# A ring of its own for the modulation weights, and squares on ScalarE, in a two-layer RWKV / band-attention trunk

## The chip, the cores and the metric

The kernel runs on one core of a Trainium2 chip. That core has a matrix engine (TensorE, "PE" in the profile, with "PEld" for its weight loads), three engines for everything else (VectorE "DVE", ScalarE "ACT", GpSimd "POOL") and a queue engine (SyncE, "SP") that issues nearly all transfers from the chip's memory. Each engine works through its own instructions in a fixed order and waits on semaphores. The metric is the device time of one execution in microseconds (us), less is better.

## The reference, cut to what matters

All arithmetic is in float32 on 256 tokens (T) with 2048 features (D). Layer 0 is an RWKV-7 time mix and an MLP, layer 1 a banded attention and an MLP. Every sub-layer is normed and modulated by vectors that come from `c`:

```python
for layer in range(DEPTH):
    mod = c @ w_ada[layer] + b_ada[layer]                     # 2048 x 12288 weights for six vectors
    sh1, sc1, gt1, sh2, sc2, gt2 = jnp.split(mod, 6, axis=-1)
    if layer == N_A_LAYERS:
        sh_kv, sc_kv = jnp.split(c @ w_ada_kv + b_ada_kv, 2, axis=-1)
        h_kv = modulate(rms_norm(x, g_kv), sh_kv, sc_kv)
        ...                                                   # shared keys and values
    h = modulate(rms_norm(x, g_mix[layer]), sh1, sc1)
    y = rwkv7_time_mix(...) if layer < N_A_LAYERS else chunk_band_attention(...)
    x = x + gt1[:, None, :] * y
    h = modulate(rms_norm(x, g_mlp[layer]), sh2, sc2)
    x = x + gt2[:, None, :] * sq_relu_mlp(h, w_up[layer], w_down[layer])
return rms_norm(x, g_final)

def sq_relu_mlp(h, w_up, w_down):
    return jnp.square(jax.nn.relu(h @ w_up)) @ w_down         # 2048 -> 8192 -> 2048
```

The modulation vectors are products of one row with large matrices: 14 vectors of 2048, each from 16 MB of weights that are used once.

## The kernel before, in words

**Layout and precision.** Activations stand with features on the 128 partitions and tokens along the free dimension, in 16 tiles of 128 x 256. A float32 product is made of reduced-precision (fp32r) parts: weights and activations are each split into a high half H and a low half L, and a product is H·H + H·L + L·H. A projection (128 output features) takes 16 contraction steps. `proj2` (L390 to L398) does a step in two matmuls: H of the weight against both halves of the activation at once (512 columns, L396), L of the weight against the high half (256 columns, L397). `proj` (L379 to L388) does it in three.

**Weights.** `weight` (L376) loads a projection's weights as two raw tiles of 128 x 1024 (512 KB). `raw` (L348) takes the tile from the ring `raw` and issues the load on SP (L352). `halves` (L355) makes H with a ScalarE cast (L362, tile `wH`) and L with a VectorE subtraction (L365, tile `wL`); both rings have `W_BUFS` = 3 tiles. The ring `raw` has `RAW_BUFS` = 6 tiles. A raw tile is free again when its subtraction is done.

**Modulation.** `ada_work` (L411) is a generator. For each half of a vector it takes 16 steps; a step loads a raw tile of 128 x 1024 modulation weights from the same ring `raw`, and VectorE adds it, scaled by one entry of `c`, to the accumulator `acc` (L423 for the first, L425 for the others). There is one `acc`. After 16 steps `ada_sum` (L432) sums it over the partitions with 32 small matmuls (L437), and VectorE adds the bias (L441). `ada` takes a step, `ada_tick` (L944) one or two per projection, and `ada_need` all that are left for the vectors named. So the steps are strewn between the projections.

**Stages** in the order of time of the profiled execution: layer A with its modulation, to about 760 us; the drain of its last head pairs, in which the output projection `w_o` is begun, and the rest of `out_proj` (L845), to about 840; MLP 0 to about 1586; `attention` (L948) with the shared keys, values and queries to about 1930; its output projection, to about 2040; MLP 1 to the end. The last modulation vector is done at about 2120.

**The MLP** (L883) has four rounds of 16 up and 16 down projections. For an up projection `sum2` (L878) adds the two halves of the PSUM result (a ScalarE copy L880 and a VectorE add L881); then VectorE makes the square of the positive part in one instruction (L904), ScalarE casts it to the high half of the hidden tile `hHL` (L905), and VectorE subtracts for the low half (L906). The first `RAW` = 4 ups of a layer work on activations that are not normed yet; `late_norm` (L527) corrects them, with the maximum in it, and L899 squares. A down projection ends in two VectorE updates of the residual `x` (L931). In the last round `scaled` (L511: L515 on ScalarE, L516 on VectorE) and `ss_add` (L477) prepare the next norm, and `rstd` (L486 to L499) and `normed_tile` (L502: L506 to L508) follow at the next stage's start.

**Attention.** `scores` (L994) loads a head's bias tile, blanks two blocks of it on GpSimd (L1000, L1001), makes the scores in PSUM, and VectorE writes scaled scores plus bias to `s` (L1006), on which the softmax works (L1010 to L1015); `weighted` transposes and multiplies with the values. A pair of heads is worked on between the quarters of a later query projection.

**What sets the order.** The program text names the work; a scheduler (the Tile framework) then sets the order of each engine's instructions before the kernel runs, from the text's order and its own estimate of when operands and buffers come free. SP's loads are in that order too. With one ring, loads stand in the order of the text, since they take its tiles in turn.

Of the kernel before, what the change touches and what calls it, by code (L numbers as in the profile page):

```python
# [2 lines left out]

# [1 line left out]

# [19 lines left out]
C = 64  # L25
# [4 lines left out]
HK = 8  # L30
# [295 lines left out]
class Body:  # L326
# [18 lines left out]
        return self.vecs[:, i, :] if kt is None else self.vecs[:, i, kt:kt + 1]  # L345


    def raw(self, src, shape=None):  # L348
        t = self.wp.tile([P, HK * P], F32, tag="raw", bufs=self.RAW_BUFS, name="raw")
        if shape is not None:  # L350
            t = t.rearrange("p (a b) -> p a b", a=shape)
        self.nc.sync.dma_start(out=t, in_=src)  # L352
        return t
# [57 lines left out]
    def ada_work(self, layer, part):  # L411
        nc = self.nc
        w, bias = self.ada_src(layer, part)
        dst = self.mods[(layer, part)]
        n_ = HK * P
        for half in range(KT // HK):
            self.fin(HK)
            acc = self.wp.tile([P, n_], F32, tag="acc", bufs=1, name="acc")
            for kt in range(KT):
                raw = self.raw(w[kt * P:(kt + 1) * P, half * n_:(half + 1) * n_])  # L420
                ck = self.ct[:, kt:kt + 1]
                if kt == 0:
                    nc.vector.tensor_scalar(out=acc, in0=raw, scalar1=ck, scalar2=0.0, op0=ALU.mult, op1=ALU.add)  # L423
                else:
                    nc.vector.scalar_tensor_tensor(out=acc, in0=raw, scalar=ck, in1=acc, op0=ALU.mult, op1=ALU.add)  # L425
# [113 lines left out]
    def run(self):  # L539
        nc, tc, d = self.nc, self.tc, self.d  # L540
        ctx = self.ctx
        gp = self.gp = ctx.enter_context(tc.tile_pool(name="gp", bufs=1))
        self.wp = ctx.enter_context(tc.tile_pool(name="wp", bufs=2))
        nc.scalar.preload_act_table_set("natural_log_exp_and_others")
        self.hp = ctx.enter_context(tc.tile_pool(name="hp", bufs=2))
        self.csts = gp.tile([P, CST.shape[1]], F32, name="csts")
        self.vecs = gp.tile([P, len(VECS), KT], F32, name="vecs")
        self.bada = gp.tile([P, 2 * 96 + 32], F32, name="bada")
        self.ct = gp.tile([P, KT], F32, name="ct")
        nc.scalar.dma_start(out=self.ct, in_=d["c"])  # L550
# [5 lines left out]
        self.lazy, self.fins = False, iter(())  # L556
        self.ada_done = set()
        self.adas = self.ada_all()

        sv, sp = ExitStack(), ExitStack()  # L560
        v = self.layer_a(sv, sp)
        with ExitStack() as st:
            self.np = st.enter_context(tc.tile_pool(name="npl", bufs=1, side="right", reuse_waits="tile"))
            xp = st.enter_context(tc.tile_pool(name="xp", bufs=1, side="right", reuse_waits="tile"))
            self.x = xp.tile([P, KT, T], F32, name="x")
            for j in range(KT - 2, KT):
                self.split(self.y_hl, j, v[:, j, :])
            sv.close()
            self.ada_need((0, 2), (0, 4), (0, 3))
            nxt = self.out_proj(self.pp, "w_o", self.y_hl, (0, 2), "g_mlp0", (0, 4), (0, 3), self.o_ps)  # L570
            sp.close()
            with ExitStack() as s2:
                pp = s2.enter_context(tc.tile_pool(name="ps_m0", bufs=2, space=bass.MemoryType.PSUM, reuse_waits="tile"))
                self.psm = lambda: pp.tile([P, 512], F32, tag="m", bufs=2, name="m")
                nxt = self.mlp(s2, pp, 0, *nxt, "g_kv", ("kv", 1), ("kv", 0))
            with ExitStack() as s2:
                pp = s2.enter_context(tc.tile_pool(name="ps_at", bufs=2, space=bass.MemoryType.PSUM, reuse_waits="tile"))
                self.psm = lambda: pp.tile([P, 512], F32, tag="m", bufs=1, name="m")
                o_hl = self.attention(s2, pp, *nxt)
                self.ada_need((1, 2), (1, 4), (1, 3))  # L580
                nxt = self.out_proj(pp, "attn_w_o", o_hl, (1, 2), "g_mlp1", (1, 4), (1, 3))
            with ExitStack() as s2:
                pp = s2.enter_context(tc.tile_pool(name="ps_m1", bufs=2, space=bass.MemoryType.PSUM, reuse_waits="tile"))
                self.psm = lambda: pp.tile([P, 512], F32, tag="m", bufs=2, name="m")
                self.mlp(s2, pp, 1, *nxt)
                r = self.rstd()
                for lo, hi, eng in ((0, 4, nc.vector), (11, 14, nc.gpsimd), (4, 8, nc.vector), (8, 11, nc.vector),
                                    (14, KT, nc.gpsimd)):
                    x = self.x[:, lo:hi, :]
                    eng.tensor_tensor(out=x, in0=x, in1=r.unsqueeze(1).to_broadcast([P, hi - lo, T]), op=ALU.mult)  # L590
                    (nc.sync if eng is nc.vector else nc.scalar).dma_start(out=d["out"][:, lo:hi, :], in_=x)
# [291 lines left out]
    def mlp(self, st, pp, layer, scaled, gain, shift, g=None, sc=None, sh=None):  # L883


        nc, tc, d = self.nc, self.tc, self.d
        hp = st.enter_context(tc.tile_pool(name=f"hid{layer}", bufs=1, reuse_waits="tile"))

        rstd, hl, nxt = self.rstd(), self.new_hl(), None

        def up(q, f):
            w = self.weight(d["w_up"][layer, q * KT + f])
            ps = pp.tile([P, 512], F32, tag="pj", bufs=3, name="pj")
            t = hp.tile([P, T], F32, tag="t", bufs=2, name="t")
            h = hp.tile([P, 2, T], F32R, tag="hHL", bufs=18, name="hHL")
            if q == 0 and f < RAW:
                self.proj(ps[:, :TE], w, lambda kt: scaled[:, kt])
                self.late_norm(t, ps, rstd, ALU.max, 0.0)
                nc.vector.tensor_tensor(out=t, in0=t, in1=t, op=ALU.mult)  # L899
            else:  # L900
                ps = ps.rearrange("p (i t) -> p i t", i=2)
                self.proj2(ps, w, lambda kt: hl[:, kt, :, 0:T])
                self.sum2(t, ps)
                nc.vector.scalar_tensor_tensor(out=t, in0=t, scalar=0.0, in1=t, op0=ALU.max, op1=ALU.mult)  # L904
            nc.scalar.copy(h[:, 0, :], t)  # L905
            nc.vector.tensor_tensor(out=h[:, 1, :], in0=t, in1=h[:, 0, :], op=ALU.subtract)  # L906
            hid.append(h)
            if q or f >= RAW:
                self.ada_tick(layer)

        for q in range(NQ):
# [13 lines left out]
            for n in range(KT):  # L925
                w = self.weight(d["w_down"][layer, q * KT + n])
# [3 lines left out]
                for i in range(2):  # L930
                    nc.vector.scalar_tensor_tensor(out=x, in0=ps[:, i, :], scalar=self.mods[(layer, 5)][:, n:n + 1],  # L931
                                                   in1=x, op0=ALU.mult, op1=ALU.add)
# [15 lines left out]
    def attention(self, st, pp, scaled, kv_gain, kv_shift):  # L948
        nc, tc, d = self.nc, self.tc, self.d
        pk = st.enter_context(tc.tile_pool(name="pat", bufs=1, reuse_waits="tile"))  # L950
# [35 lines left out]
        none = lambda: None  # L986
        turn = none
        for j in range(KT):
            t = pk.tile([P, T], F32, tag="vf", bufs=2, name="vf")
            projected(d["w_v_shared"][j], hkv, t, 1, (none, none, turn))  # L990
            turn = lambda j=j, t=t: token_major(j, t)
        o_hl = self.new_hl()
        rb = d["rb"]
        def scores(j, q):  # L994
            out = []
            for hd in range(2):
                K = slice(C * hd, C * hd + C)
                bias = pk.tile([P, 384], F32, tag="bias", bufs=4, name="bias")
                nc.sync.dma_start(out=bias, in_=rb[2 * j + hd])
                nc.gpsimd.memset(bias[0:C, C:P], -1e30)  # L1000
                nc.gpsimd.memset(bias[0:C, 320:384], -1e30)  # L1001
                S = pp.tile([P, 512], F32, tag="S", bufs=2, name="S")
                nc.tensor.matmul(S[:, 0:P], q[K, 0:P], ks[K, j, 0:P], start=True, stop=True)
                nc.tensor.matmul(S[:, P:384], q[K, P:T], ks[K, j, :], start=True, stop=True)
                s = pk.tile([P, 384], F32, tag="s", bufs=4, name="s")
                nc.vector.scalar_tensor_tensor(out=s, in0=S[:, 0:384], scalar=C ** -0.5, in1=bias,  # L1006
                                               op0=ALU.mult, op1=ALU.add)
                m = pk.tile([P, 4], F32, tag="mx", bufs=4, name="mx")
                for i, (lo, hi) in enumerate(((0, P), (P, 384))):
# [121 lines left out]
```

## Time and profile before

| | us |
|---|---|
| median of three runs | 2769.86 |
| lowest, highest | 2765.64, 2773.61 |
| the profiled execution's own time | 2776.48 |
| its span (first to last instruction) | 2774.7 |
| PE busy | 2666.3 |
| DVE busy | 2120.3 |
| ACT busy | 1277.1 |
| POOL busy | 286.7 |

The mean granted clock of TensorE in that execution is 0.986. Busy time counts instructions that work; waiting and issuing does not count. A row of a view of waits reads "who waited <- for what: us in total, times, longest". A row of the groups of lines reads "line, engine, operation, out<-in, shape, count | busy us, mean ns of one | idle us before it <- what ended that". A row of the timeline begins with its start and its length in us; what stands in brackets is the idle time before it and what ended it. Lines are those of the kernel before.

### The profile page before, as it was taken

The numbers are of one execution on the slowest core, as the hardware profiler recorded it, in microseconds if no ns is written. First come the engines' busy times: TensorE is split into PE (matmuls) and PEld (weight loads), VectorE is DVE, ScalarE is ACT, GpSimd is POOL, SyncE is SP. The second block draws the span as 40 slices with busy tenths as digits, with TensorE's granted clock in tenths as the row PEclk, the third lists the DMA queues.
The fourth block names the chain that finished last, engine by engine and source line by source line (L and its number), as shares of the span: only waits on it lengthen the run. The fifth ranks groups of instructions, "written<-read, shape, count | busy, mean of one in ns | idle before, by whom it ended". The sixth has DMA issues, their size and how long they took to land.

```text
span 2774.7 us, 58075 instructions
## 1 busy us (share of the span) xinstructions
PE 2666.3 (96%) x23594; PEld 2236.9 (81%) x23594; DVE 2120.3 (76%) x3161; ACT 1277.1 (46%) x2253; POOL 286.7 (10%) x416
## 2 busy tenths in 40 slices
PE   6999999999999999999999999998999999999997
PEld 3677777777888888888888888776888888888886
DVE  4568678788899888788888997799997566565665
ACT  2345455555445434344344454465454344443454
POOL 0003343353210000000000100000100000000002
PEclk9999999999999999999999999999999999999999
DMA  9876456554686889898898878888867555555553
GB/s 300 279 268 193 153 184 190 169 182 150 211 303 226 304 304 304 292 308 306 299 313 288 294 245 278 277 264 271 282 229 269 184 189 188 185 189 185 187 188 123
DMA packets 217389, 662.62 MB, mean 239 GB/s; under 512 B 21409, under 2 KB 68897, under 8 KB 217121
## 3 DMA queue, kind: packets, MB, share of 16 engines
q1 hardware_dynamic: 215056, 656.36, 71.3%
q8 instruction: 185, 3.03, 0.4%
q10 hardware_dynamic: 2064, 2.54, 0.3%
q14 instruction: 84, 0.68, 0.1%
HBM read 656.72 MB, written 2.10 MB: 237 GB/s over the span
## 4 chain that ended last, share of the span: by engine, by line
PE 79%; DVE 7%; DMA 6%; issue 4%; ACT 2%; POOL 1%; DVEq 0%; ACTq 0%; POOLq 0%
PE pj L396 41%; PE pj L397 21%; DMA raw<-w_ada 3%; DVE wL L365 3%; DMA raw<-w_ada_kv 2%; PE iv L105 2%; PE gr L99 1%; DVE acc L425 1%; PE m L639 1%; PE o L385 1%; PE ms L99 1%; ACT wH L362 1%; POOL sL L117 1%; PE o L387 1%; PE py L320 1%
## 5 line engine op out<-in xcount | busy, mean ns | idle before, releaser
L396 PE MATMUL pj<-aHL,wH 128*128 128x512 f32 x3520 | 1282.1, 404 | 8.7 <-ACT wH L362 6.5
L362 ACT CAST wH<-raw 128x1024 fp32r<-128x1024 f32 x772 | 807.2, 1046 | 973.2 <-PE pj L396 611.2
L365 DVE TENSOR_TENSOR wL<-raw,wH 128x1024 fp32r<-128x1024 f32 x772 | 943.6, 1225 | 270.7 <-ACT wH L362 267.8
L397 PE MATMUL pj<-aHL,wL 128*128 128x256 f32 x3520 | 993.2, 282 | 2.4 <-DVE wL L365 2.3
L396 PEld LDWEIGHTS pj<-aHL,wH 128*128 128x128 f32 x3520 | 666.5, 189 | 170.3 <-issue 10.1
L396 PE MATMUL pj<-hHL,wH 128*128 128x512 f32 x2048 | 725.4, 399 | 4.3 <-DVE hHL L906 4.3
L397 PEld LDWEIGHTS pj<-aHL,wL 128*128 128x128 f32 x3520 | 666.7, 189 | 5.6 <-DVE wL L365 4.0
L397 PE MATMUL pj<-hHL,wL 128*128 128x256 f32 x2048 | 574.6, 281 | 4.8 <-DVE wL L365 4.7
L425 DVE SCALAR_TENSOR_TENSOR acc<-raw,ct,acc 128x1024 f32<-128x1024 f32 x360 | 467.0, 1297 | 123.5 <-DMA raw<-w_ada 83.3
L396 PEld LDWEIGHTS pj<-hHL,wH 128*128 128x128 f32 x2048 | 385.3, 188 | 100.4 <-DVE hHL L906 6.7
L397 PEld LDWEIGHTS pj<-hHL,wL 128*128 128x128 f32 x2048 | 387.4, 189 | 7.1 <-DVE wL L365 6.7
L484 POOL TENSOR_TENSOR ss<-ss,sq 128x256 f32<-128x256 f32 x56 | 52.0, 929 | 1615.5 <-ACT sq L483 1615.2
L931 DVE SCALAR_TENSOR_TENSOR x<-pj,mod,x 128x256 f32<-128x256 f32 x256 | 123.2, 481 | 51.6 <-PE pj L397 48.6
L905 ACT CAST hHL<-t 128x256 fp32r<-128x256 f32 x128 | 51.6, 403 | 61.2 <-DVE t L904 60.2
L639 PE MATMUL m<-rawa,crep 128*32 128x256 f32 x512 | 47.2, 448 | 16.8 <-DMA rawa<-w_ada 16.3
L387 PE MATMUL pj<-aHL,wL 128*128 128x258 f32 x192 | 55.9, 293 | 6.9 <-DVE wL L365 6.9
L385 PE MATMUL pj<-aHL,wH 128*128 128x258 f32 x192 | 56.2, 293 | 2.2 <-ACT wH L362 1.6
L386 PE MATMUL pj<-aHL,wH 128*128 128x258 f32 x192 | 56.3, 293 | 0.0
L906 DVE TENSOR_TENSOR hHL<-t,hHL 128x256 fp32r<-128x256 f32 x128 | 53.4, 417 | 1.4 <-ACT hHL L905 1.4
L904 DVE SCALAR_TENSOR_TENSOR t<-t 128x256 f32<-128x256 f32 x120 | 50.7, 422 | 2.7
L881 DVE TENSOR_TENSOR t<-pj,t 128x256 f32<-128x256 f32 x120 | 50.0, 417 | 0.5 <-ACT t L880 0.5
L241 POOL TENSOR_TENSOR al<-da,csts 128x128 f32<-128x128 f32 x64 | 41.1, 652 | 68.8 <-PE iv L105 64.1
(246 smaller groups left out, 2792.6 us busy)
## 6 DMA issues: line engine op xcount, KB each, us to landing
raw<-w_ada SPq DMA_DIRECT2D x320, 512.0 KB, 4.9
raw<-w_up SPq DMA_DIRECT2D x256, 512.0 KB, 4.8
raw<-w_down SPq DMA_DIRECT2D x256, 512.0 KB, 4.3
rawa<-w_ada SPq DMA_DIRECT2D x64, 512.0 KB, 6.6
raw<-w_ada_kv SPq DMA_DIRECT2D x64, 512.0 KB, 5.6
raw<-w_k SPq DMA_DIRECT2D x32, 512.0 KB, 4.4
raw<-w_r SPq DMA_DIRECT2D x32, 512.0 KB, 4.6
raw<-w_o SPq DMA_DIRECT2D x32, 512.0 KB, 5.0
```

The source lines that it names most:

```text
L99: self.b.nc.tensor.matmul(o(c)[K], lhsT(c)[K], rhs(c)[K], start=True, stop=True)
L105: self.b.nc.tensor.matmul(o[QS[K], c, :], lhsT[QS[R], c, :], rhs[QS[R], c, :], start=True, stop=True, tile_position=(H * R, H * K))
L362: nc.scalar.copy(Hf, raw)
L365: eng.tensor_tensor(out=Lf, in0=raw, in1=Hf, op=ALU.subtract)
L385: nc.tensor.matmul(ps, H[:, i, :], a(kt)[:, 0, :], start=(first and kt == 0), stop=False)
L386: nc.tensor.matmul(ps, H[:, i, :], a(kt)[:, 1, :], start=False, stop=False)
L387: ins = nc.tensor.matmul(ps, L[:, i, :], a(kt)[:, 0, :], start=False, stop=(last and kt == KT - 1))
L396: nc.tensor.matmul(ps, H[:, i, :], a(kt), start=(kt == 0), stop=False)
L397: ins = nc.tensor.matmul(ps[:, 0, :], L[:, i, :], a(kt)[:, 0, :], start=False, stop=(kt == KT - 1))
L425: nc.vector.scalar_tensor_tensor(out=acc, in0=raw, scalar=ck, in1=acc, op0=ALU.mult, op1=ALU.add)
L639: nc.tensor.matmul(ps[g:g + 32, part, :W], crep[:, kt, :], raw[:, i, :], start=(part == 1 and kt < 4), stop=(part == 0 and kt >= KT - 4), ...
L931: nc.vector.scalar_tensor_tensor(out=x, in0=ps[:, i, :], scalar=self.mods[(layer, 5)][:, n:n + 1], in1=x, op0=ALU.mult, op1=ALU.add)
```

## The change

- Modulation steps can take their raw tile from a ring of their own, `rada`. The context `ada_room(n)` opens a pool with `n` such tiles; inside it `raw(..., ada=True)` uses that pool. It is open around the first output projection (5 tiles), MLP 0 (5), attention with its output projection (3) and MLP 1 (5). Before the first output projection, in layer A, modulation weights still use the ring `raw`. That ring keeps its six tiles.
- In an up projection, ScalarE takes the positive part (Relu, in place, but for the first four ups), squares it into the high half of `hHL`, and squares it once more in place in float32. VectorE no longer multiplies there; its subtraction stays.
- In attention, the bias is loaded into the tile `s` itself (ring of 5 in place of two rings of 4), and the value tiles `vf` share the ring `q` (3 tiles) in place of one of their own (2).

The scheduler makes a new order from this. In the built order of the changed kernel the loads of projection weights and of modulation weights no longer alternate as the text has them; modulation steps come in denser groups with gaps between them. No instruction is added or removed but those named.

```diff
+    @contextmanager
+    def ada_room(self, n):
+        with self.tc.tile_pool(name=f"ada_{len(self.ada_done)}", bufs=1, reuse_waits="tile") as pool:
+            self.ada_pool = pool, n
+            yield
+            self.ada_pool = None
+
+    def raw(self, src, shape=None, ada=False):
+        if ada and self.ada_pool:
+            pool, n = self.ada_pool
+            t = pool.tile([P, HK * P], F32, tag="rada", bufs=n, name="rada")
+        else:
+            t = self.wp.tile([P, HK * P], F32, tag="raw", bufs=self.RAW_BUFS, name="raw")
...
-                raw = self.raw(w[kt * P:(kt + 1) * P, half * n_:(half + 1) * n_])
+                raw = self.raw(w[kt * P:(kt + 1) * P, half * n_:(half + 1) * n_], ada=True)
...
-            nxt = self.out_proj(self.pp, "w_o", self.y_hl, (0, 2), "g_mlp0", (0, 4), (0, 3), self.o_ps)
+            with self.ada_room(5):
+                nxt = self.out_proj(self.pp, "w_o", self.y_hl, (0, 2), "g_mlp0", (0, 4), (0, 3), self.o_ps)
...
+                s2.enter_context(self.ada_room(5))
                 nxt = self.mlp(s2, pp, 0, *nxt, "g_kv", ("kv", 1), ("kv", 0))
...
+                s2.enter_context(self.ada_room(3))
                 o_hl = self.attention(s2, pp, *nxt)
...
+                s2.enter_context(self.ada_room(5))
                 self.mlp(s2, pp, 1, *nxt)
...
                 self.late_norm(t, ps, rstd, ALU.max, 0.0)
-                nc.vector.tensor_tensor(out=t, in0=t, in1=t, op=ALU.mult)
             else:
                 ps = ps.rearrange("p (i t) -> p i t", i=2)
                 self.proj2(ps, w, lambda kt: hl[:, kt, :, 0:T])
                 self.sum2(t, ps)
-                nc.vector.scalar_tensor_tensor(out=t, in0=t, scalar=0.0, in1=t, op0=ALU.max, op1=ALU.mult)
-            nc.scalar.copy(h[:, 0, :], t)
+                nc.scalar.activation(t, t, AF.Relu)
+            nc.scalar.activation(h[:, 0, :], t, AF.Square)
+            nc.scalar.activation(t, t, AF.Square)
             nc.vector.tensor_tensor(out=h[:, 1, :], in0=t, in1=h[:, 0, :], op=ALU.subtract)
...
-            t = pk.tile([P, T], F32, tag="vf", bufs=2, name="vf")
+            t = pk.tile([P, T], F32, tag="q", bufs=3, name="vf")
...
-                bias = pk.tile([P, 384], F32, tag="bias", bufs=4, name="bias")
-                nc.sync.dma_start(out=bias, in_=rb[2 * j + hd])
-                nc.gpsimd.memset(bias[0:C, C:P], -1e30)
-                nc.gpsimd.memset(bias[0:C, 320:384], -1e30)
+                s = pk.tile([P, 384], F32, tag="s", bufs=5, name="s")
+                nc.sync.dma_start(out=s, in_=rb[2 * j + hd])
+                nc.gpsimd.memset(s[0:C, C:P], -1e30)
+                nc.gpsimd.memset(s[0:C, 320:384], -1e30)
...
-                s = pk.tile([P, 384], F32, tag="s", bufs=4, name="s")
-                nc.vector.scalar_tensor_tensor(out=s, in0=S[:, 0:384], scalar=C ** -0.5, in1=bias,
+                nc.vector.scalar_tensor_tensor(out=s, in0=S[:, 0:384], scalar=C ** -0.5, in1=s,
```

More of the change, by code (lines that the diff above doesn't have):

```diff
@@ L1 @@
 import math
-from contextlib import ExitStack, nullcontext
+from contextlib import ExitStack, contextmanager, nullcontext
 import numpy as np
@@ L345, in vec @@
         return self.vecs[:, i, :] if kt is None else self.vecs[:, i, kt:kt + 1]
-    def raw(self, src, shape=None):
-        t = self.wp.tile([P, HK * P], F32, tag="raw", bufs=self.RAW_BUFS, name="raw")
+    @contextmanager
[10 more added lines that the diff above has]
+            t = self.wp.tile([P, HK * P], F32, tag="raw", bufs=self.RAW_BUFS, name="raw")
         if shape is not None:
@@ L555, in run @@
         self.nhalf, self.pool_every = 0, 0
-        self.lazy, self.fins = False, iter(())
+        self.lazy, self.fins, self.ada_pool = False, iter(()), None
         self.ada_done = set()
```

## The prediction

> **What bounds the kernel now.** I read the page first, then the busy time by stretches, then the waits and the groups of lines in the stretch that the change touches most. From the page, the busy time by engine and the chain of waits:
>
> ```profile
> PE 2666.3 (96%) x23594; PEld 2236.9 (81%) x23594; DVE 2120.3 (76%) x3161; ACT 1277.1 (46%) x2253; POOL 286.7 (10%) x416
> PE 79%; DVE 7%; DMA 6%; issue 4%; ACT 2%; POOL 1%; DVEq 0%; ACTq 0%; POOLq 0%
> ```
>
> TensorE is the bound, so only its idle time can be won: 2774.7 - 2666.3 = 108 us in all. The busy time by stretches says where it lies. The columns are the stretch, its length, then the busy time and count of PE, PEld, DVE, ACT and POOL, the granted clock, the DMA share and GB/s.
>
> ```profile
> 760.00:800.00 40.00, 34.67 (x220) 31.45 (x219) 34.00 (x43) 18.37 (x34) 7.90 (x8) 0.91 0.90 299
> 840.00:870.00 30.00, 25.61 (x189) 24.93 (x189) 27.90 (x58) 17.24 (x29) 0.00 (x0) 0.89 0.38 122
> 870.00:1580.00 710.00, 698.59 (x4548) 604.89 (x4547) 602.51 (x740) 304.57 (x392) 10.50 (x12) 1.00 0.88 302
> 1580.00:1620.00 40.00, 36.43 (x263) 33.81 (x262) 37.39 (x68) 22.39 (x36) 2.42 (x10) 1.00 0.62 204
> ...
> 1780.00:1800.00 20.00, 15.86 (x92) 12.70 (x91) 16.01 (x23) 7.58 (x16) 0.23 (x2) 1.00 0.83 287
> 1800.00:1920.00 120.00, 118.77 (x876) 91.95 (x874) 113.61 (x251) 70.42 (x195) 6.69 (x54) 1.00 0.83 275
> 1920.00:1940.00 20.00, 11.02 (x103) 7.10 (x104) 17.44 (x31) 7.54 (x18) 0.00 (x0) 0.69 0.72 228
> ...
> 2040.00:2070.00 30.00, 26.06 (x173) 24.02 (x173) 28.05 (x52) 15.69 (x27) 0.00 (x0) 0.94 0.50 160
> 2070.00:2110.00 40.00, 40.00 (x231) 34.96 (x230) 36.54 (x47) 19.31 (x29) 0.00 (x0) 1.00 0.93 331
> 2110.00:2750.00 640.00, 639.99 (x3693) 556.08 (x3693) 395.24 (x512) 280.92 (x358) 13.62 (x12) 1.00 0.58 187
> ```
>
> In order these are: the end of layer A's drain (idle 5.3 us), the start of MLP 0 (4.4), its body (11.4), the start of attention (3.6), its first softmax (4.1), its scores (1.2), its tail (9.0), the start of MLP 1 (3.9), and the rest of MLP 1 after the last modulation weights, which has nothing to win. The change cannot reach anything before about 760 us: up to there the built orders of both kernels agree but for the last loads.
>
> The waits of MLP 0's body (who waited for whom: us in total, times, longest):
>
> ```profile
> PE pj L397 <- DVE wL L365: 7.0, 7, 2.0
> PE pj L396 <- DVE hHL L906: 4.3, 3, 1.9
> DVE acc L425 <- DMA raw<-w_ada_kv: 38.9, 27, 3.4
> DVE acc L425 <- DMA raw<-w_ada: 38.6, 33, 2.1
> ACT hHL L905 <- DVE t L904: 53.0, 44, 2.9
> ```
>
> PE's 11.3 us there are VectorE's lateness, in the low halves of the weights (L365) and in the last hidden tile of an up stage (L906). VectorE is late because its queue is in order and it stands 77.5 us in front of modulation weights (L425) that have not landed; ScalarE in turn waits 53.0 us for VectorE's square.
>
> **The change part by part.** Durations come from the groups of lines of that body, ScalarE's Square from the tile view of `sq`, and the landing times from the DMA issues:
>
> ```profile
> L365 DVE TENSOR_TENSOR wL<-raw,wH 128x1024 fp32r<-128x1024 f32 x244 | 296.5, 1218 | 19.5 <-ACT wH L362 18.5
> L362 ACT CAST wH<-raw 128x1024 fp32r<-128x1024 f32 x244 | 256.4, 1051 | 340.2 <-PE pj L396 219.9 <-issue 103.1 <-DVE x L931 7.1
> L425 DVE SCALAR_TENSOR_TENSOR acc<-raw,ct,acc 128x1024 f32<-128x1024 f32 x154 | 198.1, 1286 | 78.3 <-DMA raw<-w_ada_kv 38.9 <-DMA raw<-w_ada 38.6
> L931 DVE SCALAR_TENSOR_TENSOR x<-pj,mod,x 128x256 f32<-128x256 f32 x123 | 58.8, 478 | 4.1 <-PE pj L397 3.5
> L906 DVE TENSOR_TENSOR hHL<-t,hHL 128x256 fp32r<-128x256 f32 x61 | 25.4, 417 | 0.0
> L904 DVE SCALAR_TENSOR_TENSOR t<-t 128x256 f32<-128x256 f32 x60 | 25.2, 421 | 1.0
> L483 ACT ACTIVATE sq<-x x60: 399/402/422, 773.3 to 2760.9; 128x256 f32<-128x256 f32 x60
> raw<-w_ada SPq DMA_DIRECT2D x320, 512.0 KB, 4.9
> raw<-w_up SPq DMA_DIRECT2D x256, 512.0 KB, 4.8
> ```
>
> *Squares.* 120 fused max-multiplies (421 ns) and 8 multiplies (about the same) leave VectorE: 128 x 0.42 = 54 us. ScalarE loses 128 casts and gets 120 Relu and 256 Square; at 402 ns each that is +248 x 0.402 = 100 us, 0.80 us per up projection. Relu itself is not in this trace; a Square of the same size is the nearest row. ScalarE is busy 281 of 640 us in MLP 1 and VectorE 395, PE 639.99, so there both moves cost nothing. If that cover went, the hidden tile of the last up would be late: its chain loses one engine change and gains a Square, some 0.5 us later, and the built order of MLP 1 uses that tile two matmuls later than before. I take 0, ends 0 and +2 us (four stage ends at 0.5).
>
> *Own ring.* Before, weights and modulation weights share six tiles. In the built order I add up VectorE's work between the release that lets a load go and that load's use, at the durations above: in MLP 0 the median is 5.0 us for modulation weights (a quarter under 3.8) and 8.8 for projection weights. A load lands in 4.8 to 4.9, so the former come late half the time, as the 77.5 us show. After, with five tiles of their own, the medians are 13.0 and 15.5, the lowest 5.0 and 7.8. The bytes are the same, and 331 GB/s in one stretch against 302 in the body shows some room. The body's 11.4 us of idle should mostly go. What is late next: with loads early, the scheduler bunches the modulation steps, two per projection for eight projections, then none for about four. In a run a down projection gives VectorE 2 x 1.218 + 2 x 0.478 + 2 x 1.286 = 5.96 us, an up 2 x 1.218 + 2 x 0.417 + 2 x 1.286 = 5.84. PE's pace, from two sums that are two up projections apart:
>
> ```profile
> 2232.14 0.42 DVE L881 TENSOR_TENSOR t<-pj,t 128x256 f32<-128x256 f32 x1
> ...
> 2243.36 0.41 DVE L881 TENSOR_TENSOR t<-pj,t 128x256 f32<-128x256 f32 x1
> ```
>
> is 11.22 / 2 = 5.61. VectorE falls behind by 8 x 0.35 = 2.8 us in a run of downs, 1.8 in one of ups. With three cast tiles, one comes free when PE has two (5.61 us) left to do; cast and subtraction take 1.05 + 1.22, so VectorE may be 5.61 - 2.27 = 3.3 us late. So a run should just fit, with a few tenths lost in each of the ten runs. I take 8 of the 11.4 as gained; ends 0 and 11.4.
>
> The Trainium skill (Perfetto Trace Analysis, section Identifying the Most-Contended Engine) says that matmul busy share is a poor measure of headroom and weight-load share a good one. By it the body holds 604.89 / 710 = 85.2% against 556.08 / 640 = 86.9% in the undisturbed stretch, some 14 us lost in place of 11.4, and the term would be 10 in place of 8.
>
> *Attention's tail.* There the shared ring costs most:
>
> ```profile
> 1910.38 15.98 SPq L352 DMA_DIRECT2D raw<-w_ada  x7
> 1928.48 4.84 SPq L352 DMA_DIRECT2D raw<-attn_w_o  x4
> 1930.37 3.92 DVE L425 SCALAR_TENSOR_TENSOR acc<-raw,ct,acc 128x1024 f32<-128x1024 f32 x3
> 1934.16 1.04 ACT L362 CAST wH<-raw 128x1024 fp32r<-128x1024 f32 x1 [4.17 <-DMA raw<-attn_w_o]
> 1935.26 0.80 PE L396 MATMUL pj<-aHL,wH 128*128 128x512 f32 x1 [5.68 <-ACT wH L362]
> ```
>
> Seven modulation loads fill the ring, the output projection's first weights go at 1928.48, and PE starts on them at 1935.26. After, those weights are not behind that ring, and the built order puts about 16 matmul pairs of the projection (16 x 0.35 = 5.6 us) among the last heads' small matmuls. I take the 9.0 us of idle; ends 5.7 (that one wait) and 11 (with neighbours).
>
> *Seams*, where VectorE is the limit. End of the drain: five of ten modulation steps leave the front of the first `x` updates, 5 x 1.286 = 6.4 us of VectorE; gain 3 of 5.3, ends 0 and 5.3. Start of MLP 0: four squares fewer, 4 x 0.42; gain 1, ends 0 and 2. Start of attention: three modulation steps and one more low half now stand within the last statistics and rstd, 3 x 1.286 + 1.22 = 5.1 us; with a little slack a loss of 4, ends 0 and 6. First softmax: two steps fewer ahead of it; gain 2.5, ends 0 and 4.1. Start of MLP 1: two steps and a low half within rstd, 3.8, less four squares 1.7; loss 2, ends 0 and 4. Folding the bias into `s` and `vf` into `q` changes no work: a bias load now waits for a transpose one projection earlier, whose period there is about 9 us, against 5 to land; 0.
>
> Sum: -8 - 9 - 3 - 1 + 4 - 2.5 + 2 + 0 = -17.5 us. The ends together: -34 and +6. The profiled execution took 2776.48, 6.6 us over the median of the three runs, 2769.86; I take the sum off both, 2759 for an execution like this one, 2752 for the median.
>
> **The rivals.** *The relief does not reach PE* (no change): the runs of steps use up the slack as the late loads did, the drain and the first softmax give nothing, and only the tail is won, against the seams: -9 + 4 + 2 = -3, 2767. For it speaks that 77.5 us of waits cost PE only 11. Chance 0.14.
>
> *One queue, two rings* (slower): SP still issues in one fixed order. A modulation load whose tile is held by the previous half's sum holds the projection weights behind it. The lowest weight lead of 7.8 us less 4.8 of landing leaves 3: if real release is over 3 us later than the order assumes, PE waits for the excess. At 2 us in each of some twenty halves that is 40 - 17.5 = +22, 2792. Against it: the median lead is 15.5. Chance 0.08.
>
> *ScalarE's queue becomes the limit* (slower): Relu stands ahead of a weight cast and waits for VectorE's sum, itself behind a 1.29 us step; in a run of ups each could lose 0.4 us, over MLP 0's 60 ups 25 in place of the 8 gained: -17.5 + 8 + 25 = +15, 2785. It decides once Relu's wait for VectorE, 2 x 0.40 of work and the run's lag together pass the 3.3 us. For it: ScalarE gets 0.80 more per up where it already waited 53 us. Chance 0.06. The Trainium skill (ScalarE: Activation LUTs, section Rules for kernel authors) tells to put relu, max and mul on VectorE and not ScalarE, which points this way. Here 402 against 421 ns at this size gives VectorE no advantage.
>
> **How the numbers follow.** The forecast has 0.72. Under 0.3% (8 us) a measurement here does not tell a difference. Faster 0.72, same 0.14, slower 0.14. The time is 2752; the range runs from 2738, nearly all gains, to 2775, the upper ends, which takes in the first rival.
>
> **What would show it.** Right: VectorE's waits for modulation loads in MLP 0 far below 77; PE's waits for `hHL` and `wL` there under 4 us; no idle 5.7 us ahead of the first `attn_w_o` matmul; a start of attention that is worse than before; MLP 1 unchanged. Wrong: PE waits for `wL` behind ScalarE's Relu, or weight loads that wait at SP for `acc`.

## The result

| | before | after |
|---|---|---|
| median of 13 runs, us | 2769.25 | 2759.80 |
| lowest, highest, us | 2759.08, 2774.89 | 2753.33, 2764.83 |
| span of the profiled execution, us | 2774.7 | 2751.5 |
| its own time, us | 2776.48 | 2753.33 |

The ratio of the runs is 0.9959, 95% interval 0.9949 to 0.9969: the change is faster by 0.41%, or 11.4 us of 2769, where 17.5 had been forecast.

The two profiled executions are 23 us apart, and half of that is not the change's. The rstd ahead of MLP 0 starts at 839.3 us before and at 828.2 after. That difference had arisen by about 410 us, in layer A, where both kernels do the same work in the same order: between 260 and 390 us the execution of before has 23.9 us at half the granted clock, that of after 3.4. The change has no part in that. From that rstd on, the traces can be compared. The table gives each stage's length from landmarks that both traces have: the start of an rstd's first matmul, the first copy of a key projection, and the transpose of head pair 9.

| stage | before | after | difference |
|---|---|---|---|
| MLP 0, rstd to rstd | 752.7 | 738.4 | -14.3 |
| start of attention, to the first key copy | 31.8 | 34.9 | +3.1 |
| keys, values, queries, first heads | 244.8 | 242.0 | -2.8 |
| later heads and output projection, to the next rstd | 162.8 | 164.6 | +1.8 |
| MLP 1, to the last rstd | 730.4 | 730.1 | -0.3 |

These add up to -12.5, close to the 11.4 of the ratio.

The busy time by engine and the chain of waits, from the page of after:

```profile
PE 2651.1 (96%) x23594; PEld 2231.8 (81%) x23594; DVE 2078.0 (76%) x3033; ACT 1368.1 (50%) x2501; POOL 288.3 (10%) x416
PE 84%; DVE 7%; DMA 3%; issue 3%; POOL 1%; ACT 1%; DVEq 0%; SPq 0%; ACTq 0%; POOLq 0%
```

VectorE lost 42 us of work and ScalarE gained 91. In the chain that ended last, the share of DMA fell from 6% to 3%. The busy time by stretches of after, at the places that the prediction listed for before (stretch, length, then busy time and count of PE, PEld, DVE, ACT, POOL, clock, DMA share, GB/s):

```profile
748.00:788.00 40.00, 32.16 (x217) 29.30 (x216) 34.47 (x43) 17.96 (x33) 7.01 (x8) 0.91 0.97 344
829.00:859.00 30.00, 26.62 (x196) 25.49 (x195) 27.07 (x56) 19.17 (x35) 0.00 (x0) 0.94 0.59 206
858.00:1556.00 698.00, 697.84 (x4587) 608.65 (x4586) 594.20 (x687) 352.16 (x517) 13.04 (x13) 1.00 0.88 308
1556.00:1596.00 40.00, 29.55 (x275) 28.17 (x274) 33.74 (x62) 18.66 (x31) 1.84 (x11) 0.91 0.67 223
...
1756.00:1776.00 20.00, 18.74 (x111) 15.62 (x110) 16.81 (x26) 10.16 (x21) 0.00 (x0) 1.00 0.91 318
1776.00:1890.00 114.00, 113.95 (x844) 88.94 (x843) 105.73 (x234) 68.03 (x183) 6.22 (x52) 1.00 0.81 266
1890.00:1910.00 20.00, 17.78 (x104) 12.79 (x103) 18.74 (x38) 9.45 (x27) 0.23 (x2) 1.00 0.74 242
1910.00:2008.00 98.00, 90.77 (x604) 78.04 (x603) 84.90 (x103) 44.20 (x64) 12.34 (x14) 0.93 0.79 265
2008.00:2050.00 42.00, 37.43 (x250) 35.25 (x250) 38.57 (x68) 23.64 (x42) 0.00 (x0) 0.92 0.71 241
2090.00:2727.00 637.00, 637.00 (x3689) 554.61 (x3688) 370.39 (x456) 318.56 (x463) 13.75 (x13) 1.00 0.57 184
```

The body of MLP 0 (third row) has no idle time left: 0.16 us in 698. The start of attention (fourth) got worse: 10.45 us of idle in 40 and a clock of 0.91, where before had 3.57 and 1.00. The tail of attention (1890 to 2008) still has 2.2 + 7.2 us. The waits of MLP 0 up to the rstd behind it show both sides (who waited for whom: us in total, times, longest):

```profile
ACT t L919 <- DVE t L897: 58.9, 54, 3.6
DVE acc L437 <- DMA rada<-w_ada: 12.9, 12, 2.5
DVE acc L437 <- DMA rada<-w_ada_kv: 5.5, 5, 1.9
PE m L501 <- DVE ss L496: 7.6, 1, 7.6
PE pj L409 <- DVE wL L377: 0.6, 2, 0.4
```

VectorE's wait for modulation weights fell from 77.5 to 18.4 us, and PE's for weights and hidden tiles in the body from 11.3 to under 1. ScalarE's new Relu (L919) does wait 58.9 us for VectorE's sum, but no wait of PE comes from it. New is one wait of 7.6 us for the last sum of squares (L496).

### The profile page after: what moved, and what is told of

Read it like the earlier page. It is cut to its first block, busy times and chain, and to the rows that moved or that the text cites. A ratio compares the mean times of both kernels' runs of the same rounds, so it can differ in the third digit from the quotient of the medians.

```text
span 2751.5 us, 58214 instructions
## 1 busy us (share of the span) xinstructions
PE 2651.1 (96%) x23594; PEld 2231.8 (81%) x23594; DVE 2078.0 (76%) x3033; ACT 1368.1 (50%) x2501; POOL 288.3 (10%) x416
## 4 chain that ended last, share of the span: by engine, by line
PE 84%; DVE 7%; DMA 3%; issue 3%; POOL 1%; ACT 1%; DVEq 0%; SPq 0%; ACTq 0%; POOLq 0%
PE pj L408 45%; PE pj L409 22%; DVE wL L377 2%; PE iv L105 2%; DMA rada<-w_ada 1%; PE gr L99 1%; PE m L655 1%; DVE acc L437 1%; PE ms L99 1%; PE o L397 1%; POOL sL L117 1%; PE chn L278 1%; PE py L320 1%; PE chn L285 1%; PE v L751 0%
## 5 line engine op out<-in xcount | busy, mean ns | idle before, releaser
L408 PE MATMUL pj<-hHL,wH 128*128 128x512 f32 x2048 | 717.5, 396 | 0.0
L437 DVE SCALAR_TENSOR_TENSOR acc<-rada,ct,acc 128x1024 f32<-128x1024 f32 x265 | 339.0, 1279 | 39.8 <-DMA rada<-w_ada 33.7
L496 POOL TENSOR_TENSOR ss<-ss,sq 128x256 f32<-128x256 f32 x56 | 53.1, 948 | 1592.3 <-ACT sq L495 1592.1
L437 DVE SCALAR_TENSOR_TENSOR acc<-raw,ct,acc 128x1024 f32<-128x1024 f32 x95 | 127.1, 1338 | 0.2
L919 ACT ACTIVATE t<-t 128x256 f32<-128x256 f32 x120 | 50.1, 417 | 136.2 <-DVE t L897 136.2
L921 ACT ACTIVATE t<-t 128x256 f32<-128x256 f32 x128 | 53.4, 417 | 3.3
L920 ACT ACTIVATE hHL<-t 128x256 fp32r<-128x256 f32 x128 | 52.9, 414 | 3.9 <-DVE t L543 2.8
```

The lines of the kernel that those rows point to most:

```text
L408: nc.tensor.matmul(ps, H[:, i, :], a(kt), start=(kt == 0), stop=False)
```

## The experiments

Two things had to be told apart first: which half of the change makes the gain, and whether a ring of its own does it or simply more tiles. Then came the two places where the forecast was off, the tail and the start of attention. MLP 0 is compared from rstd to rstd in single traces, whole kernels by the ratio to the kernel before. MLP 1, in whose body PE waits for nothing, still varies from 724 to 734 us among the traces shown here, so a difference of some us in one trace is taken as a sign only where the mechanism is seen too.

**The ring alone.** The change without its squares:

```diff
                 self.late_norm(t, ps, rstd, ALU.max, 0.0)
+                nc.vector.tensor_tensor(out=t, in0=t, in1=t, op=ALU.mult)
...
-                nc.scalar.activation(t, t, AF.Relu)
-            nc.scalar.activation(h[:, 0, :], t, AF.Square)
-            nc.scalar.activation(t, t, AF.Square)
+                nc.vector.scalar_tensor_tensor(out=t, in0=t, scalar=0.0, in1=t, op0=ALU.max, op1=ALU.mult)
+            nc.scalar.copy(h[:, 0, :], t)
```

> The modulation weights' own ring and the folded tiles as in the change; squares as before (VectorE squares, ScalarE casts). Theory A, the depth of the load queue made the gain: 8 to 12 us faster than before, MLP 0's body 10 to 13 us shorter between its first and last up, VectorE's waits for modulation loads in it under 20 us in place of 77. Rival B, the 54 us of VectorE work that the squares took away made it: 0 to 3 us faster, and PE's waits for wL and hHL in MLP 0 still near 11 us.

**The squares alone.** The kernel before with the `up` of the change, and nothing else of it.

> The kernel before with ScalarE's squares alone; one ring of six, nothing folded. Theory A: 0 to 4 us faster than before, the 77 us of VectorE's waits for modulation loads in MLP 0 stay above 60 (VectorE only waits longer for the same loads), PE's wait for hHL (4.3) goes, its waits for wL (7.0) stay. Rival B: 7 to 11 us faster.

Measured: the ring alone took 2759.22 us, ratio 0.9956 (0.9942 to 0.9969), as fast as the whole change. The squares alone took 2771.66, ratio 1.0011 (0.9998 to 1.0024). The ring makes the gain. The waits of MLP 0 show why the squares give nothing; from the kernel with the squares alone:

```profile
DVE acc L425 <- DMA raw<-w_ada_kv: 40.3, 25, 3.9
DVE acc L425 <- DMA raw<-w_ada: 37.7, 36, 2.6
PE pj L397 <- DVE wL L365: 10.0, 13, 2.8
```

VectorE has less work there, and waits for the same late loads: 78.0 us, 77.5 in the kernel before.

**More tiles, but one ring.** In the change, weights and modulation weights take the two pools' tiles in turn, whoever comes. That is eleven tiles in one sequence in MLP 0:

```diff
-        if ada and self.ada_pool:
+        self.nraw = getattr(self, "nraw", -1) + 1
+        if self.ada_pool and self.nraw % (self.RAW_BUFS + self.ada_pool[1]) >= self.RAW_BUFS:
```

> The change with one thing undone: inside the rooms both kinds of weights take turns through all tiles (six old and five new, three new in attention), so the loads keep to the text's alternation and only the depth is new. Theory A (depth): 8 to 14 us faster than before, as the change. Rival C (a ring of its own, so that neither kind waits for the other's tile, is what counts): 0 to 5 us faster, VectorE's waits for modulation loads in MLP 0 between 30 and 77 us.

Measured: 2766.77 us, ratio 0.9985 (0.9975 to 0.9995). Five more tiles in one ring give little more than a third of the gain, as the rival in its expectation said. That looked like a proof that the separation counts. The next two runs say otherwise.

**Own rings of 2 tiles, and of 4.** The change with another number of tiles:

```diff
-                s2.enter_context(self.ada_room(5))
+                s2.enter_context(self.ada_room(2))
```

in all four stages; and with 4 where the change has 5.

> The change with rings of 2 tiles in the four stages (instead of 5, 5, 3 and 5). If the own ring works by separation (a modulation load no longer has to find a free tile between weight tiles, and a weight tile no longer waits behind one), two tiles must do nearly the same as five: VectorE's waits for modulation loads in MLP 0 between 18 and 35 us (77 in the kernel before, 18 after the change), PE's waits for wL and hHL there under 6 us, and a time of 2759 to 2763 us. If it works by depth (more bytes on their way), two tiles give back most of it: waits of 50 us or more and a time of 2765 to 2771 us.

> The change with rings of 4 tiles (instead of 5) behind the output projection, in MLP 0 and in MLP 1; the attention keeps its 3. If what counts is how many modulation loads are on their way (with 2 tiles VectorE waited 88 us for them in MLP 0, with 2.4 of the shared six 77, with 4.4 of a shared eleven 37, with 5 of their own 18), four tiles give a wait of 37 to 50 us in MLP 0 and a time of 2764 to 2770 us. If an own ring is better than a shared one of the same depth, the wait is under 30 us and the time 2758 to 2763 us.

Measured: with two tiles 2799.78 us, ratio 1.0144 (1.0122 to 1.0166), much slower than the kernel before and than either line of its expectation; with four 2765.15, ratio 0.9985 (0.9972 to 0.9998), the same as the one ring of eleven. Their waits in MLP 0, first with two tiles, then with four:

```profile
DVE acc L437 <- DMA rada<-w_ada: 47.5, 44, 4.2
DVE acc L437 <- DMA rada<-w_ada_kv: 38.7, 31, 4.2
PE pj L409 <- DVE wL L377: 14.3, 15, 2.6
```

```profile
DVE acc L437 <- DMA rada<-w_ada: 27.9, 22, 2.4
DVE acc L437 <- DMA rada<-w_ada_kv: 17.7, 13, 2.9
```

An own ring is not good by being separate alone. What orders these five kernels is how many modulation loads can be on their way. An MLP projection takes two weight tiles and about 1.3 modulation steps (165 steps in 128 projections), so of a shared ring about 0.4 of the tiles are modulation loads (an estimate from these counts; the loads under way were not measured):

| raw tiles in MLP 0 | modulation loads under way | VectorE waits for them, us | MLP 0, us | ratio |
|---|---|---|---|---|
| own ring of 2 | 2 | 86.2 | 769.7 | 1.0144 |
| one ring of 6 (before) | 2.4 | 77.5 | 752.7 | 1 |
| own ring of 4 | 4 | 45.6 | 749.5 | 0.9985 |
| one ring of 11 | 4.4 | 37.2 | 744.0 | 0.9985 |
| own ring of 5 (after) | 5 | 18.4 | 738.4 | 0.9959 |

The waits are those of each trace from rstd to rstd (the 88 us in the expectation of four tiles were read a little further). They fall with the number of loads under way, shared and own rings alike. The ring alone, five tiles too, has 7.2 us, so kernels with the same ring differ by some ten. With two tiles of its own, VectorE is so late that PE waits 14.3 us for `wL`, 7.0 in before. An own ring of more than five tiles was not tried, so where the line ends is open. The count does not cover everything, either: in the one ring of eleven ScalarE's casts wait 12.9 us for late projection weights in MLP 0, and with the own rings of 2, 4 and 5 tiles not at all. So the separation may have a part that these runs do not single out.

**Steps earlier, for the tail.** At the end of attention the vectors that MLP 1 needs first must be complete, and nine steps are left over for that place (352 are needed there; by the order of the text 118 in layer A and the drain, 165 in MLP 0 and 60 in attention make 343). They stand in VectorE's queue ahead of the low halves of `attn_w_o`. In the change, every second value projection now takes two steps:

```diff
-            projected(d["w_v_shared"][j], hkv, t, 1, (none, none, turn))
+            projected(d["w_v_shared"][j], hkv, t, 1 + j % 2, (none, none, turn))
```

> The change, and every second value projection takes two modulation steps in place of one: eight steps more there, where VectorE has room, and eight fewer left over for the end of attention. Theory (VectorE's steps set attention's tail, so the own ring could not shorten it): 5 to 9 us faster than the change, that is 15 to 20 faster than before; the time between the last query projection and the statistics ahead of MLP 1 is shorter by as much. Rival (the tail is set by the last heads' chain of softmax, transposes and products, or by TensorE's lower clock behind it): within 3 us of the change, 8 to 14 faster than before.

Measured: 2753.16 us, ratio 0.9941 (0.9926 to 0.9956). By the ratios that is 5 us faster than the change, with intervals that overlap a little. From head pair 9 to the next rstd it takes 153.1 us (after 164.6, before 162.8), for 5.4 more in the stretch with the value projections. The tail by stretches, first of the kernel before, then of this one (the latter stretch begins some 10 us later in the work):

```profile
1890.00:1935.00 45.00, 35.09 (x278) 25.60 (x276) 42.76 (x92) 21.12 (x65) 1.56 (x12) 0.92 0.80 261
1935.00:2031.00 96.00, 95.19 (x649) 82.72 (x650) 86.28 (x103) 47.96 (x68) 11.92 (x14) 0.97 0.86 288
```

```profile
1886.00:1911.00 25.00, 23.11 (x190) 16.42 (x189) 21.02 (x50) 12.74 (x36) 1.30 (x10) 0.86 0.76 251
1911.00:2006.00 95.00, 93.29 (x590) 80.31 (x590) 85.51 (x111) 48.23 (x76) 15.57 (x14) 1.00 0.76 256
```

The idle time is 10.7 us before and 3.6 here. So the forced steps hold the tail. Whether the ring has a part in the shortening shows below, in a kernel that moves the steps and has no ring in attention.

**The ring not in attention.** The change without one line:

```diff
-                s2.enter_context(self.ada_room(3))
```

> The change without the ring in the attention (the other three stay). If the attention's ring carries a part of the gain (the first softmax and the keys, where the traces differ by 3 us, and nothing in the tail), the time is 2761 to 2765 us, and VectorE waits in the attention for raw tiles of the modulation as it did before. If the ring there only brings modulation steps that fill VectorE's queue at the wrong moment, the time is 2755 to 2759 us. If MLP 0 and its drain carry all of it, 2759 to 2761 us.

Measured: 2754.03 us, ratio 0.9962 (0.9948 to 0.9976), the same as the change within the intervals; the absolute time fits none of the lines, since the kernel before also ran faster beside it (2766.54). The attention's ring is worth nothing that shows on the whole. The trace shows two things that pull against each other. VectorE's modulation steps at the end of MLP 0, first of after, then the last one of this kernel:

```profile
1557.37 1.27 DVE L437 SCALAR_TENSOR_TENSOR acc<-rada,ct,acc 128x1024 f32<-128x1024 f32 x1
1561.98 1.28 DVE L437 SCALAR_TENSOR_TENSOR acc<-rada,ct,acc 128x1024 f32<-128x1024 f32 x1 [2.21 <-DMA rada<-w_ada]
1567.38 1.28 DVE L437 SCALAR_TENSOR_TENSOR acc<-rada,ct,acc 128x1024 f32<-128x1024 f32 x1 [0.80 <-DMA rada<-w_ada]
```

```profile
1549.02 1.27 DVE L437 SCALAR_TENSOR_TENSOR acc<-rada,ct,acc 128x1024 f32<-128x1024 f32 x1
```

With free tiles in a ring that opens with attention, the scheduler put three of attention's steps ahead of the end of MLP 0 (168 steps up to the rstd, not 165). One of them waits 2.21 us for its load in front of the last updates of `x`. Without that ring MLP 0 takes 732.0 us, not 738.4, and the start of attention 31.8, not 34.9. On the other side, from the first key copy to the transpose of head pair 9, it takes 247.6, not 242.0. The balance of some 4 us is no more than single traces differ by.

**Fewer steps at the end of MLP 0.** A second way at the same place: with the two steps in the value projections, no step in the last sixteen down projections of MLP 0, and a double step at every second projection elsewhere:

```diff
-                self.ada_tick(layer)
+                if layer or q < NQ - 1:
+                    self.ada_tick(layer)
...
-        self.ada(2 if self.nticks % 3 == 0 else 1)
+        self.ada(2 if self.nticks % 2 == 0 else 1)
```

> The change with two steps behind every second value projection, without modulation steps in the last sixteen down projections of MLP 0, and with two steps behind every second (not every third) of its other projections. If the backlog of VectorE at the end of MLP 0 is what costs the change its 5 to 8 us at the start of the attention, PE's wait for the sum of squares there (7.6 us after the change) falls under 3 us, the half clock behind it goes, and the time is 2744 to 2749 us. If VectorE has no room for them in the other rounds, the body's waits come back and the time is 2752 to 2757 us.

Measured: 2753.38 us, ratio 0.9956 (0.9941 to 0.9970), no better than the change and not better than the value steps alone. The wait for the sum of squares fell from 7.6 to 1.2 us, but VectorE's waits for modulation loads in MLP 0 are back:

```profile
DVE acc L437 <- DMA rada<-w_ada: 20.2, 16, 2.9
DVE acc L437 <- DMA rada<-w_ada_kv: 13.5, 12, 2.5
PE pj L408 <- DVE hHL L922: 4.1, 3, 1.8
```

The second line of its expectation held: five tiles feed 1.3 steps per projection; at 1.5 the waits return.

**Combinations.** The ring alone with the value steps; then the change without the ring in attention and with the value steps; then the same without the squares.

> The ring alone (squares on VectorE as before) with two modulation steps behind every second value projection. If the squares are worth nothing at either place, it is as fast as the change with those steps, 2751 to 2756 us. If VectorE's full queue makes the squares count once the ring feeds it, it is slower than that, 2757 to 2762 us, and PE's waits for wL or hHL in MLP 0 are over 10 us.

> The change without the ring in the attention and with two modulation steps behind every second value projection. If the attention's ring costs its start by pulling three of the attention's steps ahead of the last x update of MLP 0, and the tail's loss is the nine steps forced there, both go, and the time is 2746 to 2751 us. If the shared ring cannot bring the 24 steps of the value projections in time, the attention gets longer by their waits and the time is 2752 to 2758 us.

> The same without the squares on ScalarE (the ring behind the output projection and in both MLPs, two steps behind every second value projection). If the squares are worth nothing, it is within 3 us of the kernel before it in this list. If they are worth something once nothing else is in the way, it is 4 us or more slower.

Measured: 2746.64 us, ratio 0.9940 (0.9923 to 0.9957); 2749.15, ratio 0.9929 (0.9915 to 0.9943); 2755.05, ratio 0.9950 (0.9933 to 0.9967). The second is the fastest kernel here by its ratio; its interval lies below that of the change, and overlaps that of the value steps with the ring in attention (0.9941). Its trace has what was expected at the seam: 733.6 us for MLP 0, and a start of attention as before (31.8). Attention as a whole is no shorter than in the kernel before: the stretch with the value projections takes 251.2 us (before 244.8), the tail from head pair 9 on 156.9 (before 162.8), so this kernel's gain lies in MLP 0. Its tail also settles what the ring does there. Without the ring in attention the moved steps shorten the tail by 7.0 us (163.9 to 156.9), 3.4 of them net of the longer stretch ahead; with the ring by 11.5, 6.1 net. The third lies 5.9 us behind the second, which by its expectation would give the squares a worth. Their intervals overlap, and the difference in the traces lies in MLP 1 (732.5 against 726.8), in whose body no engine holds up PE. Over the four pairs of kernels with and without the squares, the ratio with them is higher by 0.0011, 0.0003 and 0.0001, and lower by 0.0021: no effect is shown.

## Why the prediction was right, and where it was not

The direction and the range were right, and the mechanism of the body was shown by the runs. The gain was a third smaller than forecast. That the total came so near is in part luck, since two errors point in opposite ways: by the stages, MLP 0 gave 14.3 us where the terms had 9 at most, and attention with its tail lost 2.1 where the terms for its start, its first softmax and its tail had a gain of 7.5. Point by point, with the idle time of PE in the stretches:

- *Own ring, body, -8 us.* 11.4 of idle became 0.2, the upper end. The slack that the runs of modulation steps were to use up was enough, and the sum of VectorE's work per projection was too high. It takes each instruction at its listed length, but the records of instructions that follow one another overlap, in the trace of before as well:

```profile
2231.00 1.23 DVE L365 TENSOR_TENSOR wL<-raw,wH 128x1024 fp32r<-128x1024 f32 x1 [1.29 <-ACT wH L362]
2232.14 0.42 DVE L881 TENSOR_TENSOR t<-pj,t 128x256 f32<-128x256 f32 x1
```

  The second starts 1.14 us after the first, which is listed with 1.23. At some 0.08 us less for each of six instructions, a projection in a run takes about 5.5 us of VectorE (an estimate from rows like these), less than PE's 5.61, and VectorE does not fall behind at all. By the same overlap the 128 squares are worth some 43 us of VectorE, not 54, which fits the 42 that it lost. The prediction also held that only idle time of PE could be won, and that was not so: over the whole of MLP 0 the same matmuls were busy for 735.75 us before and 727.24 after. The groups of the hidden-tile matmuls, first before, then after, both over the body and the end of MLP 0 (count | busy us, mean ns | idle before):

```profile
L396 PE MATMUL pj<-hHL,wH 128*128 128x512 f32 x1024 | 363.0, 399 | 4.3 <-DVE hHL L906 4.3
L397 PE MATMUL pj<-hHL,wL 128*128 128x256 f32 x1024 | 287.9, 282 | 4.8 <-DVE wL L365 4.7
```

```profile
L408 PE MATMUL pj<-hHL,wH 128*128 128x512 f32 x1024 | 357.5, 395 | 0.0
L409 PE MATMUL pj<-hHL,wL 128*128 128x256 f32 x1024 | 285.2, 279 | 0.0
```

  These are 8.2 us that the idle column does not show. In before, a wait of 1.9 us at 1498 was followed by 3.4 us at half the clock, which explains 1.7 of them; the rest is open. It is not shown to be a loss by late loads: the undisturbed stretch of MLP 1 in the same trace has means of 399 and 281 ns too. The Trainium skill (Perfetto Trace Analysis, section Identifying the Most-Contended Engine) reads weight-load share in place of matmul share, and by it the prediction had put the loss at 14 us in place of 11.4. The trace agrees in direction: that share of the body rose from 85.2% to 87.2%, a little past the 86.9% of the undisturbed stretch.
- *Attention's tail, -9 us.* This step failed: the 10.7 us of idle from the later heads to the next rstd became 9.4. The wait for `attn_w_o` went as forecast, and matmul pairs of the first output projection moved among the last heads. But the nine forced steps, which had filled the ring in front of those weights, still stood in VectorE's queue. What is late next was not asked at this place. From the timeline of after, VectorE and then PE:

```profile
1908.62 1.28 DVE L437 SCALAR_TENSOR_TENSOR acc<-rada,ct,acc 128x1024 f32<-128x1024 f32 x1
...
1910.69 1.28 DVE L437 SCALAR_TENSOR_TENSOR acc<-rada,ct,acc 128x1024 f32<-128x1024 f32 x1
...
1912.28 1.28 DVE L437 SCALAR_TENSOR_TENSOR acc<-rada,ct,acc 128x1024 f32<-128x1024 f32 x1
...
1914.91 1.22 DVE L377 TENSOR_TENSOR wL<-raw,wH 128x1024 fp32r<-128x1024 f32 x1
```

```profile
1916.17 0.58 PE L409 MATMUL pj<-aHL,wL 128*128 128x256 f32 x1 [3.19 <-DVE wL L377]
```

  Three steps and four small updates stand ahead of the low half that PE waits 3.19 us for, and the half clock behind that wait takes more. PE's waits for low halves in this stretch are 5.1 us of the 9.4; the rest is spread over smaller waits. Moving eight of the steps took the tail from 164.6 to 153.1 us, and most of that also comes without the ring in attention (163.9 to 156.9). So what held the tail was the forced steps, first in the shared ring and then in VectorE's queue, and an own ring takes away only the first.
- *Start of attention, +4 us.* Right in its cause, three modulation steps within the last statistics, and too small: +6.9 of idle, over the upper end of 6. The row of the 40 us shows why: the steps cost not only their own 3 x 1.28 = 3.8 us, one also waited 2.21 for its load, and after 7.6 us of waiting PE worked at half the clock.
- *End of the drain, -3 us.* It did not come: from the first update of `x` to the rstd it took 41.6 us before and 41.9 after, and the row of 40 us around its start has 7.8 us of idle in place of 5.3. Why is open; no run singles it out.
- *Start of MLP 0, -1; first softmax, -2.5; start of MLP 1, +2.* By idle time -1.0, -2.9 and +0.6: right within a us or two. The heads after the first softmax gave another 1.2 that had no term.
- *Squares, 0.* Right: 1.0011 alone, and no effect in the three other pairs.
- *The rivals.* "The relief does not reach PE" had the right doubt at the wrong place: it was the tail that gave nothing, and the body that gave all. "One queue, two rings" did not happen with five tiles, but a short ring is as dear as it said: with two tiles 2799.78 us, where 2792 was worked out. That the figures are near is chance, for the place is another: VectorE waits for the modulation loads, and no wait of ScalarE for a projection weight shows in MLP 0. "ScalarE's queue" did not happen: the Relu waits 58.9 us in all and 3.6 at the longest, and no wait of PE follows from it. VectorE does wait longer for ScalarE's casts in MLP 0, 69.4 us in place of 20.1, but with the ring alone, where ScalarE has no Relu, it is 61.8: that is VectorE being early, not ScalarE late.

## What to carry to other kernels

When a load is late on an in-order queue, count how many loads of its kind can be under way, and compare rings by that number first; a ring of its own with too few tiles is worse than a share of a common one. When a stall is removed by letting work start earlier, look at what that work has to pass next at the same place: here the forced steps only moved from SP's queue into VectorE's, and it took one more line, which spread them, to get a part of that gain. A pool that opens with a stage lets a scheduler pull that stage's work ahead of the seam, where the engine may have no room for it.

## What the runs showed of the hardware

The granted clock of PE changes in whole stretches of 3.41 us, and after a wait at a seam it costs again. By stretches of after, at the start of attention and in the tail:

```profile
1560.43:1563.84 3.41, 0.00 (x0) 0.00 (x0) 1.86 (x3) 0.00 (x0) 0.00 (x0) 1.00 0.79 258
1563.84:1570.67 6.83, 4.03 (x17) 3.85 (x17) 3.79 (x6) 1.38 (x4) 0.00 (x0) 0.50 0.84 288
1912.00:1915.41 3.41, 0.98 (x6) 0.52 (x4) 2.85 (x5) 1.76 (x3) 0.00 (x0) 1.00 0.98 357
1915.41:1925.65 10.24, 9.47 (x90) 7.96 (x91) 8.95 (x12) 2.09 (x4) 0.79 (x1) 0.50 0.86 291
```

A wait of 7.6 us is followed by 6.83 us at 0.50, one of 3.19 by 10.24 at 0.50, in which PE is busy 92% of the time. The Trainium skill (TensorE: Matmul & The Clock Gate, section Part 1: The HAM clock gate) says that the clock halves after at least one idle window of about 3.4 us. The lengths agree with that window; the condition does not quite, since in the window before the second drop PE was busy for 0.98 us, nearly a third. Counted on in steps of 3.41 us from these, the trace of after has nine drops between 200 and 2730 us. In the window before each of them PE was busy for at most 43%, and in each window at full clock that was not followed by a drop for at least 56%. Over the thirteen traces of this case, counted in the same way, every such window under 44% was followed by half the clock and none over 67% was; in between both occur. How many busy windows it takes to come back stays open. So a wait of 2 to 3 us in front of PE can cost, beside itself, nearly half of the 3.4 to 10 us that follow (from 1916.98 on, a pair of matmuls comes every 0.64 us in place of 0.35), and the columns of busy time show that loss as work.
